# Weight buffers 64 bytes lower, and the last transposes of x behind a weight split, in one step of a hybrid decoder layer

## The chip, the cores and the metric

One core of a Trainium2 chip runs the whole step in one launch. The metric is the device time of one execution in microseconds. It was taken three times for the kernel before: 2234.94 us in the median, from 2234.89 to 2236.98. One more execution was profiled.

## The reference

A layer updates 256 prompt tokens and 8 x 4 sample tokens (288 columns in all) of width 2048 in three steps, all in float32:

```python
x = x + 0.5 * rmsnorm(swiglu(rmsnorm(x, g[0]), ffn1_w_in, ffn1_w_out), g[1])
m, sg, sh = hybrid_mixer(rmsnorm(x, g[2]), mix_w_in, ..., mix_w_out, s_gla, s_hgrn)
x = x + rmsnorm(m, g[3])
x = x + 0.5 * rmsnorm(swiglu(rmsnorm(x, g[4]), ffn2_w_in, ffn2_w_out), g[5])

def swiglu(x, w_in, w_out):             # w_in 2048 x 11264, w_out 5632 x 2048
    gate, up = jnp.split(x @ w_in, 2, axis=-1)
    return (jax.nn.silu(gate) * up) @ w_out
```

The mixer projects to 12 heads of two gated recurrences, scans them in chunks, and projects back. The outputs are x for both groups of tokens, and the final states.

## The kernel before

Activations stand with the width on the 128 partitions and the 288 tokens along them: `x[k]` for k = 0 to 15, and `y[k]` for the output of the running sub-layer. Each float32 operand of a matmul is split into a high and a low part (`xh`, `xl` for x, `hh`, `hl` for the hidden layer, the halves `h`, `l` of a buffer `wh` for weights), and a product is three matmuls: high by high (L596), low by high (L597), high by low (L598). The moving operand is the activation (128 x 288), the stationary one the weight (128 x 128).

Weights come in units of 1024 columns: a DMA on SP's queue into one of three buffers `raw`, then the split into one of four buffers `wh`, by ACT (L100, high) and DVE (L101, low). Near the borders between sub-layers, two more buffers `wh` lie on the right side of the memory, in the pools of `Border`. `W.recent` holds the two instructions of the last split. In most blocks a unit holds 512 output columns of two k.

`block` computes 512 output columns, four column tiles f of 128, in four of five PSUM buffers. For each k but those of the last unit it runs f = 0 to 3 with three matmuls each; in the last unit it goes f by f over the two k, and `evac(f)` takes each finished tile away. A block of x has 16 k: 192 matmuls, of which 24 belong to the last unit. The feed-forward layers go over the 5632 hidden columns in 11 rounds c of 512: block `gate`, block `up`, and then for the round before four blocks `out` (o = 0 to 3) of 4 k each, which add to y. The last `out` blocks take two rounds at once (8 k). So each round has 192 matmuls in gate, 192 in up and 192 in the four output blocks. The mixer has the blocks qk0, v0, qk1, v1, hfq0, hi0, hfq1, hi1, hfq2, hfq3, gate0 to gate3 and mo0 to mo3, all with the 16 tiles `xh`, `xl` moving. The scans run among the blocks up to gate1.

Before each sub-layer the mean of the squares of x is formed (`PreNorm`): ACT squares (L425), DVE adds to `acc` (L429), `high_low` splits the sum into nh and nl (L457, L458), and two matmuls sum over the partitions (L465).

In the second feed-forward layer x itself must be turned back to tokens by rows. `turn32` does this on DVE (L716 for the prompt, L718 for the samples), one tile of x after each output block of rounds 4 to 7, and `move32` issues the DMAs from POOL's queue (L727, L731) after every fourth. `finish` adds x and the scaled output at the end. The order on each engine is not that of the code alone: instructions are placed by a scheduler as soon as their operands and the buffers allow, and `with tc.issue_after(ins)` puts what is in it behind `ins` on the engine of `ins`.

Memory is given out in the order of allocation. On the left side stand constants, `x`, `y`, `xh`, `xl`, `rt`, `rp`, `acc`, `cols`, and behind them raw, wh, and the pools of the sub-layers; the right side is filled from the top down. A tile of 288 float32 is 1152 bytes a partition (4.5 x 256), so successive tiles alternate between two places modulo 256 bytes. A half of `wh` for the second k lies 4224 bytes (16.5 x 256) behind the first, so weights alternate with k in the same way. Steps between column tiles (512 bytes), between h and l (2048), and between xh and xl (18432) are multiples of 256. So the distance between a moving tile and the weights of the same k is one number modulo 256 for all of a block.

Of the kernel before, what the change touches and what calls it, by code (L numbers as in the profile page):

```python
# [9 lines left out]
F32 = mybir.dt.float32  # L10
# [6 lines left out]
P = 128  # L17
# [113 lines left out]
def trunk_kernel(ctx, tc, x_prompt, x_sample, state_gla, state_hgrn, norm_gains, f1_in, f1_out, f2_in, f2_out,  # L131
# [6 lines left out]
    xpool = ctx.enter_context(tc.tile_pool(name="xpool", bufs=1))  # L138
# [15 lines left out]
    def act_set(func):  # L154

        if cur["set"] != tables[func]:
            ins = S.preload_act_table_set(tables[func]).ins
            for u in cur["users"]:
                order(ins, u)
            cur.update(set=tables[func], load=ins, users=[])  # L160
# [8 lines left out]
    def mmtile(name):  # L169
        return mmp.tile([P, 512], F32, name=name, tag="mm")  # L170
# [5 lines left out]
    W = Weights(tc, rawp, hlp)  # L176
# [70 lines left out]
    EARLY = 4  # L247
    x = [xpool.tile([P, T], F32, name=f"x{k}") for k in range(KT)]
# [4 lines left out]
    rt = xpool.tile([P, T], F32, name="rt")  # L253
    rp = xpool.tile([P, T], F32, name="rp")
    acc = xpool.tile([P, T], F32, name="acc")
    cols = xpool.tile([P, 32], F32, name="cols")

    def gain(i, k):
        return prm[:, i * KT + k:i * KT + k + 1]
# [218 lines left out]
    class PreNorm:  # L478
# [3 lines left out]
        def __init__(self, name, update, ahead, at):  # L482

            self.name, self.update, self.ahead, self.at, self.late = name, update, ahead, at, []
            self.tmps = None
# [25 lines left out]
    class Fill:  # L511
# [3 lines left out]
        def __init__(self, pool, name, gains, gnext, some, ahead):  # L515
            self.gnext, self.name, self.some, self.ahead = gnext, name, some, ahead

            tiles = [[[pool.tile([P, T], F32R, name=f"{name}{n}{p}{k}") for k in range(EARLY)] for p in "hl"] for n in "xy"]
            self.tiles = [list(zip(*hl)) for hl in tiles]
            self.gains = pool.tile([P, 64], F32, name=f"{name}g")[:, 0:EARLY]  # L520
            V.tensor_tensor(self.gains, gains[:, 0:EARLY], prm[:, gnext * KT:gnext * KT + EARLY], op=ALU.mult)

        def old(self):
# [125 lines left out]
    def ffn(tag, gcol, gnext, pn, before, fill=None):  # L649
# [3 lines left out]
        with ExitStack() as pools:  # L653
# [53 lines left out]
            def blocks32():  # L707

                zp = final_tiles[2]
                return (zp.tile([P, 4, 8, TS], F32, name="b32", tag="b32", bufs=2),  # L710
                        zp.tile([P, 4, TS], F32, name="bs32", tag="bs32", bufs=2))

            def turn32(src, f):
                if f == 0:
                    blocks.append(blocks32())
                V.transpose(blocks[-1][0][:, :, 2 * f:2 * f + 2, :],  # L716
                            src[:, 0:TP].rearrange("p (t q c) -> p q t c", t=2, q=4))
                V.transpose(blocks[-1][1][:, f, :], src[:, TP:T])  # L718
# [28 lines left out]
            def do_out(c, n):  # L747
                hs = [hid.pop(c + i) for i in range(n)]
                if final:
                    zt, xt = final_tiles[0:2]  # L750
                end = c + n == NCH
                if end:
                    act_set(AF.Sqrt)
                    if not final:
                        border[0].fill.old()
                for o in range(4):
                    def ev(f, ps):
                        k = 4 * o + f
                        if c == 0:
                            S.activation(y[k], ps, AF.Copy)  # L760
                        elif final and end and k == KT - 1:
                            sq = sqp.tile([P, T], F32, name="sq", tag="sq")
                            with ExitStack() as es:
                                for r in (slice(0, P), slice(P, T)):
                                    V.tensor_tensor(y[k][:, r], ps[:, r], y[k][:, r], op=ALU.add)
                                    ins = V.tensor_tensor(sq[:, r], y[k][:, r], y[k][:, r], op=ALU.mult).ins
                                    es.enter_context(tc.issue_after(ins))
                            lasts.append((sq, None))
                        else:
                            V.tensor_tensor(y[k], ps, y[k], op=ALU.add)  # L770
                        if end and not (final and k == KT - 1):
                            sq = sq_add(y[k], k, 0, KT - 2, KT - 1)
                            if k >= KT - 1:
                                lasts.append(sq)
                        if end:
                            if not final:
                                border[0].fill.new(k)
                            elif k < KT - 1:
                                z = fp.tile([P, T], F32, name="z", tag="z", bufs=4)
                                S.activation(z, y[k], AF.Copy, scale=gcol(k))  # L780
                                if o < 3:
                                    turn32(z, f)
                                    if f == 3:
                                        move32(o, *zt, (G, nc.sync) if o == 2 else (G,))
                                else:
                                    if f > 1:
                                        by_token(zs[f - 2], k - 2, *zt)
                                    zs.append(z)
                    block(f"out{tag}_{c}_{o}", 4 * n, lambda k: [t[:, k % 4, :] for t in hs[k // 4]], ev,
                          tail=2 if end and o == 3 else 1, hold=end and o == 3)  # L790
                    k = 4 * (c - 4) + o
                    if final and 0 <= k < KT:
                        turn32(x[k], o)
                        if o == 3:
                            move32(c - 4, *xt, (G,))

# [20 lines left out]
    def finish(last, rest, zt, xt):  # L817

        (zT, zS), (xT, xS) = zt, xt
        mss = [mmtile(f"postf{t}") for t in range(2)]  # L820
        rc = [cols[:, 8 * t:8 * t + 1] for t in range(3)]

        def total(cols, t, start, stop):
            return PE.matmul(mss[t % 2][:, t:t + 1], cols, onesD[:, 0:1], start=start, stop=stop, skip_group_check=True).ins

        def scale(t):
            ins = act(rc[t], mss[t % 2][:, t:t + 1], AF.Sqrt, bias=epst)
            V.reciprocal(rc[t], rc[t])
            return ins

        for sq in (acc, last):
            for t in range(2):
                total(sq[:, t * P:(t + 1) * P], t, sq is acc, sq is last)
        scale(0)
        scale(1)
        four = []
        for sq in (acc, last):
            r = sqp.tile([P, 4, TS], F32, name="sq4", tag="pn")
            G.tensor_copy(r, sq[:, TP:T].unsqueeze(1).broadcast_to([P, 4, TS]))
            four.append(r.rearrange("p a b -> p (a b)"))  # L840
        for i in range(2):
            tot = total(four[i], 2, False, i == 1)
        behind = scale(2)
        rest(behind, tot)

        def add(o, z, x, t):
            V.scalar_tensor_tensor(o, z, rc[t], x, op0=ALU.mult, op1=ALU.add)  # L847

        outs = [(hlp if s else rawp).tile([P, 2, 512], F32, name=f"o{s}", tag="wh" if s else "raw") for s in range(4)]

        def prompt(s, t):
            k, o = slice(4 * s, 4 * s + 4), outs[s][:, t]
            add(o.rearrange("p (k c) -> p k c", c=P), zT[:, k, t], xT[:, k, t], t)
            nc.sync.dma_start(y_prompt[0, t * P:(t + 1) * P, s * 512:(s + 1) * 512], o)

        for t in range(2):
            for s in range(3):
                prompt(s, t)
        add(zS, zS, xS, 2)
        for q in range(4):  # L860
            S.dma_start(y_sample[:, :, q * 512:(q + 1) * 512].rearrange("b t c -> (b t) c"), zS[q * TS:(q + 1) * TS, :])
        for t in range(2):
            prompt(3, t)
# [772 lines left out]
    class Border:  # L1636


        def __init__(self, n, gains, gnext, some, ahead=0):
            self.pools = ExitStack()  # L1640
            top = self.pools.enter_context(tc.tile_pool(name=f"top{gnext}", bufs=1, side="right"))
            top.tile([P, 40], F32, name=f"gap{gnext}")
            W.begin_extra(self.pools.enter_context(tc.tile_pool(name=f"hx{gnext}", bufs=2, side="right")), wider(n))
            self.fill = Fill(self.pools.enter_context(tc.tile_pool(name=f"fl{gnext}", bufs=1, side="right")),
                             f"fill{gnext}", gains, gnext, some, ahead)
# [47 lines left out]
```

## Time and profile before

| | us |
|---|---|
| median of 3 runs | 2234.94 |
| profiled execution | 2236.25 |
| its span, first to last instruction | 2234.5 |
| PE busy | 2220.9 |
| DVE busy | 1386.0 |
| ACT busy | 1021.1 |
| POOL busy | 180.2 |

The span is what the profiler saw between the first and the last instruction; 1.75 us lie around it. A busy time counts the union of an engine's instructions, so PE is at 99% whether one matmul follows the other every 131 ns or every 133. How quick it is shows in the starts: the timeline lists each instruction with its start in us, and the start of a block's first matmul is where TensorE left the block ahead. Names in rows leave out the buffers' numbers: `up<-xh,wh` is a matmul of block up with xh moving and a weight buffer stationary. `gate` names the blocks of both feed-forward layers and of the mixer's gates.

### The profile page before, as it was taken

To read this page: it belongs to the slowest core of one execution; us is meant where nothing else is said; L and a number is where in the kernel's file an instruction comes from. 1 tells how busy PE (TensorE), PEld (TensorE's weight loads), DVE (VectorE), ACT (ScalarE), POOL (GpSimd) and SP (SyncE) were. 2 spreads that over 40 slices of the span, in tenths; PEclk is the share of its full clock that TensorE was granted. 3 is DMA by queue.
4 is the path that set the end of the run, shared out by engine and by line. 5 is a ranking of instruction groups with operands and counts; after the bars stand their busy time and mean duration, and the time that the engine had idled before them with its cause. 6 is when DMAs were issued, how large, how long until landed. Compare 5 with 4: busy or idle time off the path is not lost. (4 is left out here: it accounts for less than half of the span.)

```text
span 2234.5 us, 43195 instructions
## 1 busy us (share of the span) xinstructions
PE 2220.9 (99%) x17820; PEld 2206.3 (99%) x17820; DVE 1386.0 (62%) x2254; ACT 1021.1 (46%) x1535; POOL 180.2 (8%) x327
## 2 busy tenths in 40 slices
PE   9999999999999999999999999999999999999998
PEld 9999999999999999999999999999999999999998
DVE  7545545555555568888888755944555455545646
ACT  6443333333334345655676654543333333333344
POOL 2000000000000001233210000530000000000005
PEclk9999999999999999999999999999999999999999
DMA  7555555555555554667566554765555555555555
GB/s 223 171 164 169 167 166 168 168 164 169 168 163 180 176 164 140 194 202 214 170 188 178 175 180 132 194 184 165 170 166 165 170 166 166 168 167 166 169 163 158
DMA packets 227334, 384.87 MB, mean 172 GB/s; under 512 B 21362, under 2 KB 60864, under 8 KB 227136
## 3 DMA queue, kind: packets, MB, share of 16 engines
q1 hardware_dynamic: 213776, 364.89, 54.6%
q0 software_dynamic: 10992, 16.77, 2.8%
q8 instruction: 140, 2.29, 0.4%
q10 hardware_dynamic: 2368, 0.44, 0.1%
q14 instruction: 58, 0.48, 0.1%
HBM read 363.75 MB, written 11.80 MB: 168 GB/s over the span
## 5 line engine op out<-in xcount | busy, mean ns | idle before, releaser
L101 DVE TENSOR_TENSOR wh<-raw,wh 128x1024 fp32r<-128x1024 f32 (+1 forms) x676 | 821.7, 1216 | 621.1 <-ACT wh L100 619.4
L100 ACT ACTIVATE wh<-raw 128x1024 fp32r<-128x1024 f32 (+1 forms) x676 | 711.3, 1054 | 967.7 <-PE gate L598 302.1
L596 PE MATMUL gate<-xh,wh 128*128 128x288 f32 x1660 | 487.8, 295 | 0.0
L598 PE MATMUL gate<-xh,wh 128*128 128x288 f32 x1660 | 486.1, 294 | 0.0
L597 PE MATMUL gate<-xl,wh 128*128 128x288 f32 x1660 | 484.3, 294 | 0.0
L598 PE MATMUL up<-xh,wh 128*128 128x288 f32 x1408 | 415.9, 295 | 0.0
L597 PE MATMUL out<-hl,wh 128*128 128x288 f32 x1408 | 415.9, 295 | 0.0
L597 PE MATMUL up<-xl,wh 128*128 128x288 f32 x1408 | 415.3, 295 | 0.0
L596 PE MATMUL up<-xh,wh 128*128 128x288 f32 x1408 | 414.9, 295 | 0.0
L598 PE MATMUL out<-hh,wh 128*128 128x288 f32 x1408 | 412.2, 293 | 0.0
L596 PE MATMUL out<-hh,wh 128*128 128x288 f32 x1408 | 411.9, 293 | 0.0
L596 PEld LDWEIGHTS gate<-xh,wh 128*128 128x128 f32 x1660 | 311.3, 188 | 0.4
L598 PEld LDWEIGHTS gate<-xh,wh 128*128 128x128 f32 x1660 | 311.4, 188 | 0.2 <-DVE wh L101 0.2
L597 PEld LDWEIGHTS gate<-xl,wh 128*128 128x128 f32 x1660 | 310.7, 188 | 0.5
L596 PEld LDWEIGHTS up<-xh,wh 128*128 128x128 f32 x1408 | 265.0, 188 | 0.0
L596 PEld LDWEIGHTS out<-hh,wh 128*128 128x128 f32 x1408 | 264.8, 188 | 0.0
L597 PEld LDWEIGHTS out<-hl,wh 128*128 128x128 f32 x1408 | 264.4, 188 | 0.0
L598 PEld LDWEIGHTS up<-xh,wh 128*128 128x128 f32 x1408 | 264.4, 188 | 0.0
L598 PEld LDWEIGHTS out<-hh,wh 128*128 128x128 f32 x1408 | 264.3, 188 | 0.0
L597 PEld LDWEIGHTS up<-xl,wh 128*128 128x128 f32 x1408 | 264.1, 188 | 0.0
L770 DVE TENSOR_TENSOR y<-out,y 128x288 f32<-128x288 f32 x287 | 120.7, 452 | 90.7 <-PE out L598 89.6
L727 POOL DMA_DIRECT2D zT<-b x40 | 23.3, 588 | 716.9 <-issue 716.5
(410 smaller groups left out, 2565.9 us busy)
## 6 DMA issues: line engine op xcount, KB each, us to landing
raw<-in_ffn_w_in_dram SPq DMA_DIRECT2D x350, 512.0 KB, 3.7
raw<-in_ffn_w_out_dram SPq DMA_DIRECT2D x176, 512.0 KB, 3.7
raw<-in_mix_w_in_dram SPq DMA_DIRECT2D x64, 512.0 KB, 4.2
raw<-in_mix_w_in_dram SPq DMA_DIRECT2D x96, 256.0 KB, 3.3
raw<-in_mix_w_out_dram SPq DMA_DIRECT2D x32, 512.0 KB, 3.7
out_dram<-s POOLq DMA_DIRECT2D x32, 256.0 KB, 3.0
s<-in_state_gla_dram SPq DMA_DIRECT2D x16, 256.0 KB, 5.4
s<-in_state_hgrn_dram SPq DMA_DIRECT2D x16, 256.0 KB, 5.3
```

What stands on the lines that cost most here:

```text
L100: i1 = self.nc.scalar.activation(h[:, a, c], raw[:, a, c], AF.Copy).ins
L101: i2 = self.nc.vector.tensor_tensor(l[:, a, c], raw[:, a, c], h[:, a, c].bitcast(F32), op=ALU.subtract).ins
L596: yield lambda: PE.matmul(dst, w[0][:, a, c], parts[0], start=start, stop=False)
L597: yield lambda: PE.matmul(dst, w[0][:, a, c], parts[1], start=False, stop=False)
L598: yield lambda: PE.matmul(dst, w[1][:, a, c], parts[0], start=False, stop=stop)
L727: queues[n % len(queues)].dma_start(dst[q * TS:(q + 1) * TS, 4 * g:4 * g + 4, :, cols].rearrange("p k t c -> p (k t) c"), b32[rows, q])
L770: V.tensor_tensor(y[k], ps, y[k], op=ALU.add)
```

## The change

`cols`, the last tile ahead of the weight buffers, is cut from 128 to 64 bytes a partition. So all that follows on the left side lies 64 bytes lower: raw, wh, hh, hl and the rest. On the right side a gap at the top grows by 64 bytes, so that the two extra buffers wh lie 64 bytes lower too, and the tile behind them shrinks by 64, so that the copies of the first four tiles of x and y for `Fill` stay where they were. The places of the first byte modulo 256, for even k (odd k: 128 further):

| | before | after |
|---|---|---|
| weights (wh) | 64 | 0 |
| x moving (xh, xl, and the tiles of Fill) | 64 | 64 |
| hidden layer moving (hh, hl) | 128 | 64 |
| x less weights | 0 | 64 |
| hidden layer less weights | 64 | 64 |

And the transposes of x in rounds 4 to 7 are put behind the last weight split on DVE.

```diff
-    cols = xpool.tile([P, 32], F32, name="cols")
+    cols = xpool.tile([P, 16], F32, name="cols")
...
-            self.gains = pool.tile([P, 64], F32, name=f"{name}g")[:, 0:EARLY]
+            self.gains = pool.tile([P, 48], F32, name=f"{name}g")[:, 0:EARLY]
...
                     if final and 0 <= k < KT:
-                        turn32(x[k], o)
+                        with tc.issue_after(W.recent[1]):
+                            turn32(x[k], o)
...
-        rc = [cols[:, 8 * t:8 * t + 1] for t in range(3)]
+        rc = [cols[:, 4 * t:4 * t + 1] for t in range(3)]
...
-            top.tile([P, 40], F32, name=f"gap{gnext}")
+            top.tile([P, 56], F32, name=f"gap{gnext}")
```

The order of instructions changes at three places. DVE, where the sum of squares ahead of the second feed-forward layer ends (x_101 and x_102 are tiles 7 and 8 of x, the numbers behind wh and raw those of the units):

```order
-L429 TENSOR_TENSOR acc<-acc,sq 128x288
-L718 STREAM_TRANSPOSE bs_21109<-x_101 128x32
+L429 TENSOR_TENSOR acc<-acc,sq 128x288 x4
+L101 TENSOR_TENSOR wh_16498<-raw_16374,wh_16498 128x2x512
 L429 TENSOR_TENSOR acc<-acc,sq 128x288 x2
-L101 TENSOR_TENSOR wh_16498<-raw_16374,wh_16498 128x2x512
-L429 TENSOR_TENSOR acc<-acc,sq 128x288 x3
 L101 TENSOR_TENSOR wh_16527<-raw_16415,wh_16527 128x2x512
-L429 TENSOR_TENSOR acc<-acc,sq 128x288
 L458 TENSOR_TENSOR nl<-acc,nh 128x288
-L716 STREAM_TRANSPOSE b_21908<-x_102 128x4x64
 L101 TENSOR_TENSOR wh_16573<-raw_16456,wh_16573 128x2x512
```

The transposes are gone from here, and the last additions to acc stand ahead of the split of wh_16527, not behind it. PE at the same place, in the last unit but one of block up of round 0:

```order
 L598 MATMUL up_0_3_16336<-xh_125,wh_16412 128x288
 L465 MATMUL pre_16556<-nh,onesR 128x288
+L465 MATMUL pre_16556<-nl,onesR 128x288
 L596 MATMUL up_0_0_16333<-xh_126,wh_16453 128x288
 L597 MATMUL up_0_0_16333<-xl_142,wh_16453 128x288
 L598 MATMUL up_0_0_16333<-xh_126,wh_16453 128x288
-L465 MATMUL pre_16556<-nl,onesR 128x288
 L596 MATMUL up_0_1_16334<-xh_126,wh_16453 128x288
```

The product of nl moves three matmuls ahead, straight behind that of nh. DVE in output round 4 of the second layer, from the end of block 0 into block 1:

```order
 L770 TENSOR_TENSOR y_110<-out_4_0_3_20245,y_110 128x288
 L101 TENSOR_TENSOR wh_20303<-raw_20191,wh_20303 128x2x512
+L716 STREAM_TRANSPOSE b_20308<-x_94 128x4x64
+L718 STREAM_TRANSPOSE bs_20309<-x_94 128x32
 L770 TENSOR_TENSOR y_111<-out_4_1_0_20312,y_111 128x288
 L101 TENSOR_TENSOR wh_20340<-raw_20240,wh_20340 128x2x512
```

Here the pair of transposes of tile 0 of x (x_94) now stands, behind a split and ahead of the next block's first addition to y; the other 15 pairs follow in the same way, one a block, through round 7.

## The prediction

> **What bounds the kernel now.** I read the page first: its engine totals and the granted clock.
>
> ```profile
> span 2234.5 us, 43195 instructions
> ...
> PE 2220.9 (99%) x17820; PEld 2206.3 (99%) x17820; DVE 1386.0 (62%) x2254; ACT 1021.1 (46%) x1535; POOL 180.2 (8%) x327
> ...
> PEclk9999999999999999999999999999999999999999
> ```
>
> TensorE is busy for 99% of the span at full clock. So the kernel ends when its stream of matmuls ends, and only two things can move the end: fewer waits of TensorE, or a shorter time from one matmul to the next. The waits are few. Windows over two quiet stages, one in each feed-forward layer (columns: the stretch, its length, busy time and count of PE and PEld, then DVE, ACT, POOL, the clock, the DMA share, GB/s):
>
> ```profile
> 200.00:300.00 100.00, 100.00 (x762) 100.00 (x761) 55.07 (x75) 36.51 (x40) 0.00 (x0) 1.00 0.56 167
> ...
> 1900.00:2000.00 100.00, 100.00 (x761) 100.00 (x761) 52.53 (x68) 37.62 (x44) 0.00 (x0) 1.00 0.56 167
> ```
>
> That is 100/761 = 131.4 ns for one matmul of 288 columns, without a gap, and DVE, ACT and DMA have slack. So I looked for differences inside this 131 ns. The groups by line do not help: they give every matmul 293 to 295 ns, because matmuls overlap and their ends are modelled. Starts do help. From the timeline (columns: start us, duration us, engine, line, instruction) I took the first matmul of each block of one round, and the first of the last unit of two of them; then the same round in the other layer.
>
> ```profile
> 365.71 0.29 PE L596 MATMUL gate<-xh,wh 128*128 128x288 f32 x1
> ...
> 387.79 0.30 PE L596 MATMUL gate<-xh,wh 128*128 128x288 f32 x1
> ...
> 390.96 0.29 PE L596 MATMUL up<-xh,wh 128*128 128x288 f32 x1
> ...
> 413.22 0.29 PE L596 MATMUL up<-xh,wh 128*128 128x288 f32 x1
> ...
> 416.42 0.29 PE L596 MATMUL out<-hh,wh 128*128 128x288 f32 x1
> ...
> 441.60 0.29 PE L596 MATMUL gate<-xh,wh 128*128 128x288 f32 x1
> ...
> 1740.42 0.29 PE L596 MATMUL gate<-xh,wh 128*128 128x288 f32 x1
> ...
> 1765.67 0.29 PE L596 MATMUL up<-xh,wh 128*128 128x288 f32 x1
> ...
> 1791.12 0.29 PE L596 MATMUL out<-hh,wh 128*128 128x288 f32 x1
> ...
> 1816.31 0.29 PE L596 MATMUL gate<-xh,wh 128*128 128x288 f32 x1
> ```
>
> Gate, up and the four output blocks hold 192 matmuls each (16 k x 4 column tiles x 3). They take 25.25, 25.46 and 25.18 us in the first layer, and 25.25, 25.45 and 25.19 us in the second: 131.5, 132.6 and 131.2 ns a matmul. The pattern repeats to 0.01 us over 1375 us of other work, so it belongs to TensorE's own stream and not to what other engines happen to do. There are two rhythms: a slow one (up: 22.26 us for the first 168 matmuls, 132.5 ns) and a faster one (gate: 22.08 us for 168, 131.4 ns; out). Gate and up read the same tiles of x from the same places and use the same four weight buffers; they differ in what ran ahead. Gate comes behind an output block, up behind gate.
>
> Output blocks differ from both by the distance between the moving tile and the weights that are read beside it: 64 bytes modulo 256, against 0 for x. The last output pair of a layer (8 k deep, 96 matmuls) shows what that distance does over a longer stretch: its first matmul, the first of its last unit, and the first of the next block.
>
> ```profile
> 808.46 0.29 PE L596 MATMUL out<-hh,wh 128*128 128x288 f32 x1
> ...
> 817.92 0.29 PE L596 MATMUL out<-hh,wh 128*128 128x288 f32 x1
> ...
> 821.06 0.29 PE L596 MATMUL out<-hh,wh 128*128 128x288 f32 x1
> ```
>
> 72 matmuls in 9.46 us are 131.4 ns; the last 24, where the weights of one column tile go over two k, take 3.14 us, 130.8 ns. Up's last 24 took 3.20 us. I find no output block in the slow rhythm.
>
> **The change, part by part.**
>
> *64 bytes.* No instruction is added or removed. Everything behind x in memory moves 64 bytes down, so every product of x (gate, up, all projections of the mixer) gets the distance that output blocks have; hh and hl move with the weights and keep theirs. If distance sets the rhythm, an x block costs 168 x 9.46/72 + 3.14 = 22.07 + 3.14 = 25.21 us.
>
> - 22 up blocks at 25.455: 22 x 0.245 = 5.4 us.
> - 18 gate blocks of rounds 2 to 10 at 25.25: 18 x 0.04 = 0.7 us.
> - The four gate blocks of rounds 0 and 1, which no clean row shows: between 0.04 and 0.245 each. I take 0.1, so 0.4 us.
>
> The mixer's last blocks run without a scan beside them:
>
> ```profile
> 1253.23 0.29 PE L596 MATMUL gate<-xh,wh 128*128 128x288 f32 x1
> ...
> 1278.67 0.29 PE L596 MATMUL mo<-xh,wh 128*128 128x288 f32 x1
> ...
> 1304.12 0.29 PE L596 MATMUL mo<-xh,wh 128*128 128x288 f32 x1
> ...
> 1330.30 0.29 PE L596 MATMUL mo<-xh,wh 128*128 128x288 f32 x1
> ...
> 1355.76 0.29 PE L596 MATMUL mo<-xh,wh 128*128 128x288 f32 x1
> ```
>
> - gate3 (25.44), mo0 (25.45), mo2 (25.46) and mo3, which I take to be alike, are slow: 4 x 0.24 = 1.0 us. mo1 (26.18) holds a wait, and gate2 has no row of its own; 0.1 each, 0.2 us.
> - Twelve more blocks (qk0 to gate1) run among the scans:
>
> ```profile
> 1000.00:1100.00 100.00, 100.00 (x1085) 96.16 (x1085) 87.02 (x201) 62.72 (x146) 22.15 (x35) 1.00 0.66 190
> ```
>
> Small matmuls break the rhythm there, and DVE is at 87%, so a quicker TensorE may only wait longer for it. Bounds: 0 (all swallowed) to 12 x 0.245 = 2.9 us. The nearest rows of undisturbed work are gate's and up's, whose mean is 0.14 a block, 1.7 us; I take half of that, 0.8 us, for the 87%.
>
> *The transposes of x held back.* Without the hold they stand early on DVE, between the sums of squares of the third norm. The timeline where that sum ends, and the groups of lines between 1404 and 1440 us (count | busy us, mean ns | idle before):
>
> ```profile
> 1429.53 0.29 PE L598 MATMUL up<-xh,wh 128*128 128x288 f32 x1
> 1429.60 0.44 ACT L457 ACTIVATE nh<-acc 128x288 fp32r<-128x288 f32 x1 [1.33 <-DVE acc L429]
> ...
> 1430.08 0.46 DVE L458 TENSOR_TENSOR nl<-acc,nh 128x288 fp32r<-128x288 f32 x1 [0.51 <-ACT nh L457]
> ...
> 1430.10 0.40 PE L465 MATMUL pre<-nh,onesR 128*128 128x288 f32 x1 [0.28 <-ACT nh L457]
> ```
>
> ```profile
> L716 DVE STREAM_TRANSPOSE b<-x 128x256 f32<-128x256 f32 x9 | 3.8, 418 | 0.0
> L718 DVE STREAM_TRANSPOSE bs<-x 128x32 f32<-128x32 f32 x9 | 1.8, 195 | 0.0
> ```
>
> TensorE starts its next matmul 0.57 us after the last one, where 0.13 is usual: 0.44 us lost, since nh waits for acc and DVE has spent 3.8 + 1.8 us on transposes here. By the new order the last two sums stand ahead of a weight split (wh_16527) instead of behind it, so nh can be ready about 1 us earlier. What is late next: the product of nl, which now comes straight after that of nh and not three matmuls later. If nl is late by its own 0.46 us nothing is won; if it is in time, 0.44 and some 0.1 of a broken rhythm are. Bounds: a loss of 0.1 to a gain of 0.55; I take 0.4, since the nearest row is the wait itself, and it goes.
>
> In their new place each pair of transposes follows a weight split in output rounds 4 to 7; behind them in DVE's queue stands the next block's first addition to y. One round there, the transposes over the whole kernel (median in the middle of the three durations), POOL's longest wait for want of work, and its issues for them:
>
> ```profile
> 1791.10:1816.30 25.20, 25.20 (x194) 25.20 (x193) 18.63 (x33) 9.86 (x12) 0.00 (x0) 1.00 0.54 167
> ```
>
> ```profile
> L716 DVE STREAM_TRANSPOSE b<-x x16: 403/407/446, 1412.2 to 1449.0; 128x256 f32<-128x256 f32 x16
> ```
>
> ```profile
> POOL zT L727 <- issue: 716.5, 1, 716.5
> ```
>
> ```profile
> L727 POOL DMA_DIRECT2D xT<-b x64 | 37.3, 588 | 179.7 <-ACT sq L425 170.8 <-DVE bs L718 6.0 <-DMA xS<-bs 1.4
> ```
>
> DVE is busy for 18.63 of 25.20 us; four pairs add 4 x (0.41 + 0.20) = 2.4 us to 6.6 us of slack. The cover is the four weight buffers: a unit is 24 matmuls, 3.15 us, and a split that comes 0.6 us later still lies units ahead of its use. Without that cover it would cost up to 16 x 0.6 = 9.8 us; I put it at nothing. The DMAs that carry the result (64 of xT, and a quarter as many of xS) move on POOL's queue into the 716 us in which it waited, ahead of those of zT; the last are issued two rounds before the end, and only the last additions read them. DMA at 54% there leaves the loads of weights room. Smaller `cols` only moves three columns: nothing.
>
> Sum: 5.4 + 0.7 + 0.4 + 1.0 + 0.2 + 0.8 + 0.4 = 8.9 us. The profiled execution took 2236.25 us, 1.75 more than its span, so it would take 2227.35. The median of the runs shown, 2234.94, lies 1.31 lower; against it the sum gives **2226.0 us**.
>
> **The rivals.**
>
> 1. *Distance does nothing (0.08).* TensorE's rhythm comes from what ran ahead, and output blocks are quick because their k loop is short. For it: gate and up differ by 0.2 us at one and the same distance. Against it: 72 matmuls in a row at distance 64 stay at 131.4. Only the 0.4 us of the hold is left: 2234.5. The Trainium skill, page "SBUF — State Buffer", section "Who interferes with whom", says the same: the moving operand and the weight load have independent read ports, and TensorE never waits on anyone, so by it the places cannot matter and the sum would be the hold alone. No run here shows those ports; the rows above only show a pace that changes with no wait on another engine.
> 2. *Half of it (0.10).* The slow rhythm survives at the new distance where a block is entered out of it, in half of the up and mixer blocks. Then half of 5.4 + 1.0 + 0.2 + 0.4 + 0.8 = 3.9, with gate's 0.7 and the hold's 0.4, gives 5.0: 2229.9.
> 3. *Slower: the weights' own place counts (0.10).* All quick blocks of this trace read weights that begin at 64 or 192 modulo 256; no row shows weights at 0 or 128, where they go now. If that place holds the slow rhythm, whatever moves beside it, gates go from 25.25 to 25.455 (18 x 0.205 = 3.7 us) and the 22 output rounds from 25.18 to 25.455 (22 x 0.275 = 6.0 us). With the hold's 0.4: 2234.94 + 9.3 = 2244.2. It decides at the first output block behind an up block: over 131.5 ns there, and all blocks follow. Against it: up is slow already with its weights at 64, so the place alone does not set the rhythm.
>
> **How the numbers follow.** The forecast has 0.72: predicted 2226.0. Its own range is 2224 (scans give 2.9) to 2228 (scans and hold give nothing, the mixer's last blocks half). With rival 2 it reaches to 2232, where the two hold 0.82. A measurement of this kernel can tell 0.2%, 4.5 us, from no change. Faster by more: the forecast, and half of rival 2 as it lies near 2230.5: 0.77. Within: the other half and rival 1: 0.13. Slower: rival 3, 0.10.
>
> **What would show it.** In the profile after: up blocks at 25.2 us from first matmul to first matmul, like gate; mo0 and mo2 at 25.2; output rounds still 25.18; the wait of `pre` on nh gone, and transposes of x between 1790 and 2050 us. The forecast is wrong if up stays at 25.4 (rival 1 or 2), if output rounds pass 25.3 (rival 3), or if the scan stage from 850 to 1230 us grows by as much as the rest shrinks.

## The result, and the profile after

The changed kernel takes 2228.09 us in the median of 6 runs (2226.28 to 2229.44), against 2235.02 us before on the same chip: ratio 0.9966, 95% interval 0.9954 to 0.9978. Run a second time (5 runs) it took 2227.30 against 2235.88: 0.9964, 0.9951 to 0.9976. The forecast was 2226.0 in a range of 2224 to 2232. The profiled execution of the first set took 2226.28 us. Its page:

```profile
span 2224.5 us, 43196 instructions
...
PE 2212.8 (99%) x17820; PEld 2197.9 (99%) x17820; DVE 1386.7 (62%) x2254; ACT 1020.1 (46%) x1535; POOL 180.2 (8%) x327
```

TensorE runs the same 17820 matmuls and is busy 8.1 us less. The timeline of the changed kernel, first matmul of each block (start us, duration us), at the places shown of before:

```profile
363.46 0.29 PE L596 MATMUL gate<-xh,wh 128*128 128x288 f32 x1
...
388.67 0.29 PE L596 MATMUL up<-xh,wh 128*128 128x288 f32 x1
...
413.89 0.29 PE L596 MATMUL out<-hh,wh 128*128 128x288 f32 x1
...
439.06 0.29 PE L596 MATMUL gate<-xh,wh 128*128 128x288 f32 x1
...
1274.05 0.29 PE L596 MATMUL mo<-xh,wh 128*128 128x288 f32 x1
...
1299.26 0.29 PE L596 MATMUL mo<-xh,wh 128*128 128x288 f32 x1
...
1324.62 0.29 PE L596 MATMUL mo<-xh,wh 128*128 128x288 f32 x1
...
1349.83 0.29 PE L596 MATMUL mo<-xh,wh 128*128 128x288 f32 x1
```

Gate takes 25.21 us (25.25 before), up 25.22 (25.46), the output round 25.17 (25.18); mo0 and mo2 take 25.21 (25.45). Gate and up no longer differ, as far as the rounded starts tell: each x block outside the scans and without a wait runs in the quick rhythm. mo1 went from 26.18 to 25.36, but most of that is a wait which is not the same in every execution: mo1 took 25.21 in the second profile of the changed kernel, and 25.91 in the one of e1, which has the same places.

The scan stage, from the first matmul of v0 to that of the gate2 of the mixer; first of before, then of the changed kernel:

```profile
870.30 0.29 PE L596 MATMUL v<-xh,wh 128*128 128x288 f32 x1
...
1226.71 0.30 PE L596 MATMUL gate<-xh,wh 128*128 128x288 f32 x1
```

```profile
866.32 0.30 PE L596 MATMUL v<-xh,wh 128*128 128x288 f32 x1
...
1222.43 0.29 PE L596 MATMUL gate<-xh,wh 128*128 128x288 f32 x1
```

356.41 us became 356.11. Windows over this stage (columns as in the prediction), before and after:

```profile
870.30:1226.71 356.41, 355.20 (x3698) 343.32 (x3697) 301.37 (x669) 222.47 (x489) 84.83 (x150) 1.00 0.67 192
```

```profile
866.32:1222.43 356.11, 354.70 (x3698) 342.89 (x3697) 301.35 (x669) 222.60 (x489) 84.87 (x150) 1.00 0.67 192
```

TensorE is busy for all but 1.2 us of it before, and for all but 1.4 us after.

The third norm in the changed kernel, where TensorE lost 0.44 us before, and the rows half a round later:

```profile
1423.20 0.29 PE L598 MATMUL up<-xh,wh 128*128 128x288 f32 x1
...
1423.32 0.30 PE L465 MATMUL pre<-nh,onesR 128*128 128x288 f32 x1
...
1423.46 0.29 PE L465 MATMUL pre<-nl,onesR 128*128 128x288 f32 x1
```

```profile
1430.53 0.29 PE L598 MATMUL gate<-xh,wh 128*128 128x288 f32 x1
1430.86 0.19 PEld L596 LDWEIGHTS gate<-xh,wh 128*128 128x128 f32 x1 [0.27 <-DVE u L681]
1430.86 0.40 PE L596 MATMUL gate<-xh,wh 128*128 128x288 f32 x1
...
1431.10 0.30 PE L597 MATMUL gate<-xl,wh 128*128 128x288 f32 x1
```

The wait for nh is gone, and nl is in time. DVE is not alone in this: on ACT, too, the last four squares (L425) now stand ahead of weight splits (L100) that they stood behind. But seven microseconds later gate of round 1 waits for DVE to empty a PSUM buffer of up (L681): 0.33 us between two starts, then 0.24 to the next, where 0.13 is usual. This wait did not stand there before: gate of round 1 took 25.28 us then, and takes 25.52 now. The transposes of x, and DVE in the round that was shown of before:

```profile
L716 DVE STREAM_TRANSPOSE b<-x x16: 436/438/440, 1791.8 to 2037.4; 128x256 f32<-128x256 f32 x16
```

```profile
1783.00:1808.20 25.20, 25.20 (x195) 25.20 (x194) 20.03 (x39) 9.91 (x12) 0.00 (x0) 1.00 0.55 167
```

They run in output rounds 4 to 7, at no cost to TensorE: DVE is busy for 20.0 us of 25.2, with three of the pairs in this window.

The two profiled executions differ by 10.0 us, more than the medians (6.9 us in the first set, 8.6 in the second). By stages: rounds 2 to 10 of both layers 5.14 (657.80 to 655.23 us each), rounds 0 and 1 of both 1.6, scans 0.3, gate2 and gate3 0.34, mo0 to mo3 1.5. The other 1.0 us lies at the start and the end. Of mo's 1.5, 0.58 is mo1's wait; so 8.3 us are left to the change, between the two pairs of medians.

Whether the distances of the places bring all of this about is what the experiments ask.

### The profile page after: what moved, and what is told of

Its sections match the earlier page's. It is cut to its first block, busy times and chain, and to the rows that moved or that the text cites. A ratio compares the mean times of both kernels' runs of the same rounds, so it can differ in the third digit from the quotient of the medians.

```text
span 2224.5 us, 43196 instructions
## 1 busy us (share of the span) xinstructions
PE 2212.8 (99%) x17820; PEld 2197.9 (99%) x17820; DVE 1386.7 (62%) x2254; ACT 1020.1 (46%) x1535; POOL 180.2 (8%) x327
## 5 line engine op out<-in xcount | busy, mean ns | idle before, releaser
L100 ACT ACTIVATE wh<-raw 128x1024 fp32r<-128x1024 f32 (+1 forms) x676 | 711.0, 1053 | 961.0 <-PE gate L598 301.8
L727 POOL DMA_DIRECT2D xT<-b x64 | 37.2, 588 | 764.8 <-PE gate L598 571.8
```

The source lines that it names most:

```text
L100: i1 = self.nc.scalar.activation(h[:, a, c], raw[:, a, c], AF.Copy).ins
L727: queues[n % len(queues)].dma_start(dst[q * TS:(q + 1) * TS, 4 * g:4 * g + 4, :, cols].rearrange("p k t c -> p (k t) c"), b32[rows, q])
```

## The experiments

Distance below is the place of the moving tile less that of its weights, modulo 256 bytes. In the first four, the order of instructions on every engine is that of before (e1, e3) or of the changed kernel (e2, e4).

**e1, the layout alone.** The changed kernel without the hold:

```diff
-                        with tc.issue_after(W.recent[1]):
-                            turn32(x[k], o)
+                        turn32(x[k], o)
```

> The 64 bytes alone, without the hold of the transposes. Distance theory (the distance between the moving tile and the weights modulo 256 sets TensorE's rhythm): up, gate and the clean mixer blocks at 25.21 us as in the changed kernel, the wait of 0.57 us for nh stays; 8 to 9 us faster than before, about 2226.5. If the hold carried a good part of the gain, up stays near 25.45 and the time is within 2 us of before.

Measured 2227.40 us against 2235.60; 0.9965 (0.9952 to 0.9977). First matmuls of up and of the output round:

```profile
388.73 0.29 PE L596 MATMUL up<-xh,wh 128*128 128x288 f32 x1
...
413.94 0.29 PE L596 MATMUL out<-hh,wh 128*128 128x288 f32 x1
```

Up takes 25.21 us. The 64 bytes bring the whole gain. The wait for nh stays, but is shorter than expected: 0.39 us between two starts, not 0.57.

**e2, the hold alone.** The kernel before with the hold:

```diff
-                        turn32(x[k], o)
+                        with tc.issue_after(W.recent[1]):
+                            turn32(x[k], o)
```

> The hold alone, all places as before. Distance theory: up at 25.45, gate at 25.25; only the wait for nh goes, 0.3 to 0.5 us: 2234.5. If the hold carried the gain: below 2230.

Measured 2235.14 against 2235.60; 0.9999 (0.9990 to 1.0008): no difference that can be told. Up is as slow as before:

```profile
390.71 0.29 PE L596 MATMUL up<-xh,wh 128*128 128x288 f32 x1
...
416.17 0.29 PE L596 MATMUL out<-hh,wh 128*128 128x288 f32 x1
```

From the first matmul of gate of round 0 to that of round 2 in the second layer, the stretch with the third norm, the timelines give 130.81 us before, 130.62 with the hold alone, 130.03 with the layout alone, and 130.00 and 130.14 with both. So the hold is worth 0.2 us alone, and nothing beside the layout: the wait it removes comes back as the wait for PSUM.

**e3, distance 0 at other places.** From the kernel before:

```diff
     omlb = const.tile([P, 8], F32, name="omlb")
+    const.tile([P, 48], F32, name="pad")
...
-            top.tile([P, 40], F32, name=f"gap{gnext}")
+            top.tile([P, 56], F32, name=f"gap{gnext}")
```

> From the kernel before: x, weights, hidden layer and the rest of the left side 192 bytes higher, the right side's tiles 64 lower, so weights stand at 0 modulo 256 as in the changed kernel, but x stands at 0 too: distance 0, weights at 0. Output blocks keep distance 64. Distance theory: the slow rhythm is back, up 25.45, mo 25.45, gate 25.25, about 2235. Place theory (weights at 0 are what helps): up 25.21 and about 2226.5.

Measured 2235.07 against 2235.60; 0.9999 (0.9990 to 1.0008). The timeline (its lines stand one further down):

```profile
365.71 0.29 PE L597 MATMUL gate<-xh,wh 128*128 128x288 f32 x1
...
390.96 0.29 PE L597 MATMUL up<-xh,wh 128*128 128x288 f32 x1
...
416.41 0.29 PE L597 MATMUL out<-hh,wh 128*128 128x288 f32 x1
...
441.60 0.29 PE L597 MATMUL gate<-xh,wh 128*128 128x288 f32 x1
```

25.25, 25.45, 25.19: the blocks of before to 0.01 us, with weights at 0 as in the changed kernel. So at distance 0 the place of the weights does not set the pace; only the distance is common to the two kernels.

**e4, the hidden layer at distance 0.** The changed kernel with padding ahead of the hidden layer's tiles:

```diff
+            pools.enter_context(tc.tile_pool(name=f"pad{tag}", bufs=1)).tile([P, 48], F32, name=f"pad{tag}")
             fp = pools.enter_context(tc.tile_pool(name=f"ffn{tag}", bufs=2))
```

> The changed kernel with 192 bytes of padding ahead of the hidden layer, so hh and hl stand at 0 modulo 256, distance 0 from the weights; x keeps 64. Distance theory: output rounds grow from 25.18 to between 25.3 (gate's pace at distance 0) and 25.5 (up's), 22 times: 2.6 to 7 us slower than the changed kernel, 2230.7 to 2235; gate behind these slower output blocks stays at 25.21. Theory that a rhythm is carried over from what ran ahead: output rounds stay at 25.18, or gate behind them goes to 25.45.

Measured 2235.84 against 2235.60; 1.0001 (0.9992 to 1.0010): 8 us slower than the changed kernel.

```profile
365.05 0.29 PE L596 MATMUL gate<-xh,wh 128*128 128x288 f32 x1
...
387.30 0.29 PE L596 MATMUL gate<-xh,wh 128*128 128x288 f32 x1
...
390.44 0.29 PE L596 MATMUL up<-xh,wh 128*128 128x288 f32 x1
...
415.65 0.29 PE L596 MATMUL out<-hh,wh 128*128 128x288 f32 x1
...
441.07 0.29 PE L596 MATMUL gate<-xh,wh 128*128 128x288 f32 x1
```

Output rounds take 25.42 us, as the distance theory said. Up keeps 25.21. But gate, also at distance 64, now takes 25.39. Behind an output block at distance 0 its first 168 matmuls (to the row at 387.30) take 22.25 us, 132.4 ns each, the pace of up before; its last unit takes 3.14 us, and up behind it is quick. So distance 64 has two rhythms as well, and which one a block takes depends on the block ahead. Both theories were half right.

The same rows allow a closer reading. Before, gate at distance 0 ran its first 168 matmuls in 22.08 us, the quick pace. So at either distance a block can run most of its length at either pace. The pace changes around the last unit, where the matmuls go f by f: behind a last unit at distance 0 the next x block is slow (up before, gate in e4), behind one at distance 64 it is quick. This is read from these rows; no run tests it by itself.

**The changed kernel again**, in one chip session with the next three:

> The changed kernel once more. Adding up the stages of the two traces that a rhythm or the hold explains, and leaving out the start, the end and a wait in mo1 that differ between any two executions, the change is worth 8.4 us: about 2227, ratio 0.9962 to 0.9968. If the 10.0 us of the first pair of profiles were all due to the change: 2225.5.

2227.30 against 2235.88, as told above. It lies in the first expectation.

**e5 to e8 and e10 to e12, other distances for all products.** Each is the changed kernel with other sizes for `cols`, the gap and `gains`, and a padding ahead of the hidden layer, so that x and the hidden layer stay at 64 modulo 256 and the weights move. For distance 32:

```diff
-    cols = xpool.tile([P, 16], F32, name="cols")
+    cols = xpool.tile([P, 24], F32, name="cols")
...
-            self.gains = pool.tile([P, 48], F32, name=f"{name}g")[:, 0:EARLY]
+            self.gains = pool.tile([P, 56], F32, name=f"{name}g")[:, 0:EARLY]
...
-            fp = pools.enter_context(tc.tile_pool(name=f"ffn{tag}", bufs=2))
+            pools.enter_context(tc.tile_pool(name=f"pad{tag}", bufs=1)).tile([P, 56], F32, name=f"pad{tag}"); fp = pools.enter_context(tc.tile_pool(name=f"ffn{tag}", bufs=2))
...
-            top.tile([P, 56], F32, name=f"gap{gnext}")
+            top.tile([P, 48], F32, name=f"gap{gnext}")
```

The four sizes (cols, gains, padding, gap) are 72, 40, 8, 64 for 96; 64, 32, 16, 72 for 128; 56, 88, 24, 16 for 160; 48, 80, 32, 24 for 192; and 40, 72, 40, 32 for 224. For distance 80 the sizes are those of 96, and the halves begin 16 bytes further into each buffer:

```diff
-        h, l = hl[:, :, 0:512], hl[:, :, 512:1024]
+        h, l = hl[:, :, 4:516], hl[:, :, 516:1028]
```

> The changed kernel with the weights at 192 modulo 256 and the hidden layer padded to 64, so that every product has distance 128. If the distance counts modulo 128, this is distance 0 again for all blocks: up and, by the run with the hidden layer at 0, output rounds and gate too in the slow rhythm, 25.4 a block, 2238 to 2242. If it counts modulo 256 and only equal places collide: as the changed kernel, 2227.

> Weights at 128, hidden layer at 64, every product at distance 192, the mirror of 64. If the distance counts modulo 128: as the changed kernel, blocks of 25.21, about 2227. If it counts modulo 256, or its sign does: another rhythm, over 25.3 a block, 2231 or more.

> Weights at 32, hidden layer at 64, every product at distance 32. If equal places collide in steps of 64 bytes or coarser, 32 lies half in the collision: slow blocks, 25.3 to 25.5, 2231 to 2240. If any distance but 0 will do: 25.21, 2227. A rhythm quicker than 131.3 ns a matmul would be new.

> Weights at 224, hidden layer at 64, every product at distance 96. Distances 0, 32, 128 and 192 have given blocks of x of 25.2 to 25.5, 25.62, 25.53 and 25.55 us, 64 has given 25.21. If the quick place is one narrow step, 96 is slow too: 25.4 to 25.6, 2243 to 2257. If the quick range reaches from 64 towards 128: 25.2 or less, at or under 2227.

> Weights at 96, hidden layer at 64, every product at distance 224. Narrow-step theory: 25.4 to 25.6 a block of x, 2243 to 2257. If 64 is quick because the two reads then lie a quarter apart in a period of 256, 224 is no better than 192 (25.55).

> Weights at 160, hidden layer at 64, every product at distance 160, between 128 (25.53) and 192 (25.55). Both theories: 25.5 to 25.6, 2250 to 2256. Under 25.3 would mean that the pace depends on something else than the distance.

> As with distance 96, but the high and low halves begin 16 bytes further into each weight buffer, so weights stand at 240 and every product has distance 80, between the two quick ones: 64 (25.21 us a block of x, 131.3 ns a matmul) and 96 (25.22). If quickness is a range from 64 to 96: 25.2 or a little less, 2226 to 2228. If only multiples of 32 bytes are quick, since 16-byte steps break the reads: 25.3 or more, over 2232.

What was measured; the blocks are those of one round of the first layer, from first matmul to first matmul:

| distance | weights at | gate, up us | output round us | median us | ratio to before |
|---|---|---|---|---|---|
| 0, x alone (before) | 64 | 25.25, 25.45 | 25.18 (at 64) | 2235 to 2236 | 1 |
| 32 (e7) | 32 | 25.62, 25.62 | 25.52 | 2257.11 | 1.0096 (1.0081 to 1.0111) |
| 64 (changed) | 0 | 25.21, 25.21 | 25.17 | 2227.30 | 0.9964 (0.9951 to 0.9976) |
| 80 (e12) | 240 | 25.46, 25.46 | 25.52 | 2247.67 | 1.0054 (1.0040 to 1.0068) |
| 96 (e8) | 224 | 25.22, 25.22 | 25.20 | 2229.07, one run | against 2235.87 |
| 128 (e5) | 192 | 25.53, 25.53 | 25.47 | 2250.26 | 1.0066 (1.0052 to 1.0079) |
| 160 (e11) | 160 | 25.63, 25.63 | 25.55 | 2257.17, one run | against 2235.87 |
| 192 (e6) | 128 | 25.55, 25.55 | 25.57 | 2253.91 | 1.0081 (1.0067 to 1.0095) |
| 224 (e10) | 96 | 25.54, 25.54 | 25.52 | 2253.86, one run | against 2235.87 |

The rows at distance 32, one of the two slowest, and at 96, the second quickest:

```profile
368.68 0.30 PE L596 MATMUL gate<-xh,wh 128*128 128x288 f32 x1
...
394.30 0.30 PE L596 MATMUL up<-xh,wh 128*128 128x288 f32 x1
...
419.92 0.30 PE L596 MATMUL out<-hh,wh 128*128 128x288 f32 x1
```

```profile
363.76 0.29 PE L596 MATMUL gate<-xh,wh 128*128 128x288 f32 x1
...
388.98 0.29 PE L596 MATMUL up<-xh,wh 128*128 128x288 f32 x1
...
414.20 0.29 PE L596 MATMUL out<-hh,wh 128*128 128x288 f32 x1
```

The first window of the prediction, now at distance 32: in these 100 us TensorE runs 753 matmuls, where it ran 762 before, both at a granted clock of 1.00.

```profile
200.00:300.00 100.00, 100.00 (x753) 100.00 (x752) 54.96 (x76) 36.55 (x40) 0.00 (x0) 1.00 0.56 166
```

At each distance the pace repeats from block to block. 32 and 128 fit none of the theories offered for them: 128 is not 0 over again (25.53 where 0 gives 25.25 and 25.45), and 32 is slower than either neighbour and slower than its forecast of slow blocks. 192 is no mirror of 64, but another rhythm over 25.3, as the second theory for it said. 96 is quick, so the quick place is not one step; 80 between them is slow, so it is not a plain range either. 224 is slow as expected, and so is 160, a little past its forecast. e12 differs from the others in one more thing: its weights begin at a multiple of 16 bytes and not of 32. Whether its distance or that start makes it slow is not told apart. Nor do these runs separate distance from the weights' place as e3 does for 0; for 64 the output blocks do, which ran at 25.18 with weights at 64 and at 25.17 with weights at 0. Distances are told modulo 256 throughout because that number is the same for a whole block; that the pace repeats after 256 bytes no run shows.

No version beat the changed kernel: e1 is level with it, and 96 has blocks longer by 0.01 to 0.03 us, and its one run a mo1 that is 1.6 us longer than mo0.

## Why the prediction was right

- **What bounds the kernel.** Right: DVE, ACT, DMA and the order on TensorE stay as they were, and the time falls where block lengths fall.
- **The distance sets the rhythm.** Right for what was forecast: 25.21 us a block was worked out from 72 matmuls of an output block, and 25.21 came. e1 and e2 show that the layout alone does it, e3 that it is the distance and not the weights' place. The step was incomplete: e4 shows two rhythms at distance 64, too. In e4 the slow one came behind a block at distance 0, and the changed kernel has none left. The rows ahead of the change showed only the quick one at 64; that the other did not come up was in part luck.
- **Up and gate blocks.** Forecast 5.4 and 0.7. In rounds 2 to 10 each up gave 0.24 and each gate 0.04 us, as forecast.
- **Rounds 0 and 1.** Mis-sized: forecast 0.4 us for four gates. The first profile has 0.20 and 0.15 in the first layer, nothing and a loss of 0.24 in the second, the wait for PSUM. But the gains are no work of the change: the very first gate took 29.19 us before and 28.99 after, but also 28.96 in e2 with the places of before; and gate of round 1 took 25.56 in the second profile of the changed kernel, as it did before.
- **The mixer's last blocks.** Forecast 1.2; measured 0.12 for gate2, 0.22 for gate3, 0.24 each for mo0 and mo2, 0.23 for mo3, and 0.24 for mo1 beside its wait: 1.3.
- **The scan stage.** Mis-sized: forecast 0.8, measured 0.3. The bound at nothing was the nearer one. The reason given, a wait for DVE at 87%, is hardly what the windows show: TensorE idles 1.4 us there, against 1.2 before. Its steps from one block matmul to the next, without those over 150 ns, average 132.1 ns before and 131.8 after, while the slow rhythm has 132.5 and the quick one 131.4: before the change these blocks were not all slow, and after it not all quick. What sets their pace among the scans' small matmuls stays open.
- **The hold.** Mis-sized: forecast 0.4, measured 0.2 alone and nothing on top of the layout. The prediction named nl as what could be late next; nl was in time, and up's PSUM buffers were late instead (0.27 us for DVE's L681).
- **Not forecast.** The output block behind up is 0.01 us shorter, 0.2 us in all, since it is no longer entered out of the slow rhythm: in e3, with weights at 0 as in the changed kernel but a slow up ahead, the output round still took 25.18.
- **The rivals.** The first (distance does nothing) falls with e1. The Trainium skill, page "SBUF — State Buffer", section "Who interferes with whom", says that the moving operand and the weight load have independent read ports and that TensorE never waits on anyone. By it the layout would have been worth nothing; it was worth 8 us, and at distance 32 the kernel takes 30 us more than at 64. In the window of e7 shown above no wait of TensorE for another engine is listed, and yet it is slower. The measurement decides; by what mechanism the places act no run shows. The second rival's mechanism exists (e4), but not in this kernel. The third (the weights' place) falls with the changed kernel itself, whose output rounds take 25.17 with weights at 0; e3 bears it out.
- **The number.** 2226.0 against 2228.09 and 2227.30. The first lies just past 2228, the upper end of the forecast's own range, the second inside it. Scans, hold and the gates of rounds 0 and 1 were taken some 1.3 us too high, the mixer's last blocks and the output rounds 0.3 too low. That leaves 7.9 of the 8.9 us, between the 6.9 and 8.6 of the two pairs of medians; single executions of the changed kernel spread over 3 us.

## What to carry to other kernels

When one engine is busy for the whole span and nothing it waits for can go, compare the starts of equal blocks: durations of overlapped instructions hid a difference of 1% that starts showed to 0.01 us. In a kernel bound by float32r matmuls with a weight load each, the distance between moving tile and weights modulo 256 bytes belongs to the layout: lay it out so that all products share one good distance, since the pace of a block depends on the block ahead of it too, and measure a few, since the neighbours of a good one can be the worst. Of a stall removed from a chain, ask what is late next, and look for it some microseconds further down.

## What the runs showed of the hardware that was not expected

A stream of 128 x 128 x 288 matmuls with nothing to wait for runs at 131.1 to 133.5 ns each (25.17 to 25.63 us for 192), by the places of its operands alone. At one and the same distance there can be two stable rhythms: at 0, the first 168 matmuls of a block took 22.08 us (gate) or 22.26 (up); at 64, 22.25 in gate of e4, where up's whole block took 25.21. A rhythm keeps for over 160 matmuls and depends on the block ahead. The pace does not simply rise or fall with the distance: 32 slow, 64 quick, 80 (with a start off 32 bytes) slow, 96 quick, 128 to 224 slow. But for 0 and 64, the weights' own place moves along with the distance, and the two are not told apart.
